# A decoder layer in fp32: buffers of the MLP taken strictly in turn, a longer tail by token blocks, and a shorter inverse root

## The chip, the cores and the metric

The kernel runs on one core of a Trainium2 chip. The core has five engines that work side by side: TensorE (PE in the profile, with the weight load PEld beside it), VectorE (DVE), ScalarE (ACT), GpSimd (POOL) and SyncE (SP), which here issues the transfers. Each engine works its own instructions off in the order in which they were written for it. The metric is the device time of one execution in microseconds, lower is better; the time before is the median of three runs.

## The reference

One decoder layer on 2048 tokens of width 1024, in fp32:

```python
# token mixing: projection, differential attention + mLSTM heads, output projection
x1 = x + rmsnorm(mix(rmsnorm(x, g_mix_pre)), g_mix_post)
# channel mixing: hidden width 4096, squared ReLU
h  = rmsnorm(x1, g_mlp_pre)
u  = square(relu(h @ w_up))
y  = x1 + rmsnorm(u @ w_down, g_mlp_post)

def rmsnorm(x, g):
    return x * lax.rsqrt(mean(x * x, axis=-1) + 1e-6) * g
```

The change touches the end of the token mixing (the inverse root in the output projection) and the whole of the channel mixing.

## The kernel before, in words

**Products.** An fp32 operand is split into two fp32r parts, high and low: ScalarE makes the high part by a cast, VectorE the low part by a subtraction, and a product is three matmuls (high·high, high·low, low·high) of 128x128 by 128x512, all issued by `product` at line 962. The two matrix products of the MLP are done in Strassen's manner with seven smaller products each, numbered 1 to 7.

**Output projection** (`out_proj`). Per block of 128 tokens `project` multiplies, `residual` normalises twice with `rsqrt_act` and writes x1 to DRAM, and `spread` transposes the result and forms the seven right operands `B` of the up projection; those that don't stay in SBUF go through two buffers `hl` to DRAM (`Bd`).

**Up projection** (`MlpUp`). For two halves of the tokens (g) and eight pairs of row blocks each, the products go in the order 1, 2, 6, 7, 5, 3, 4, always for two row blocks together. Weights are loaded into `wr`, split into `w`, multiplied into the PSUM tiles `A` and `B`, squared into `u` (with `s` as a helper) and stored to DRAM as `ud`. The pools hold 5 `s`, 15 `u`, 14 `wr`, 6 `w`, 4 `A` and 4 `B`. `Rotation` (line 820) hands out tiles from up to two pools in turn; within one pool the scheduler may give a new tile any buffer that is free.

**Down projection** (`mlp_down`). The products go in the order 1, 6, 5, 3, 2, 7, 4, each over 16 blocks j. For each block `operands(i, j)` loads `ar` (line 1169) from `ud`, casts it to `ao` (ScalarE, line 1171), subtracts for the low part of `ao` (VectorE, line 1146, the helper `tt`); `right(i, j)` loads one to four pieces `br` of the weights (line 1152), combined by `tt` where there is more than one (none, 2, 1, none, none, 1, 3 subtractions or additions for products 1, 6, 5, 3, 2, 7, 4); the result is cast to `bo` (line 1175) and its low part subtracted. Then eight token blocks b get three matmuls each, into the eight PSUM tiles `pd`: 24 matmuls a block. With a product's last block, `take` empties each `pd`: a copy on ScalarE (line 1186) for products 1, 6, 5, 3, an addition to `y` on VectorE for 2, 7, 4. Buffers: 4 `ar`, 5 `ao`, 5 `bo`, 14 `br`, 6 `x1`. All loads of the stage are issued by SP in one queue, in the order of the program as the scheduler wrote it.

**The end.** The last four blocks of the last product (`TAIL`) are done the other way round: all four operand pairs are made first, then each token block gets its 12 matmuls at once, followed by its own `take`, `sumsq` (line 1199: square on ScalarE with its sum; line 1200: times the gain on GpSimd) and `finish`: sum of the two halves `ss`, `rsqrt_act` (lines 180 to 186), scaling (line 1223 on ScalarE with the addition of x1 on GpSimd, line 1224; line 1226 on VectorE for the other half) and the stores of the output (line 1227).

## Time and profile before

| | us |
|---|---|
| median of three runs (2589.5, 2590.0, 2593.72) | 2590.0 |
| the profiled execution | 2593.08 |
| its span | 2591.3 |
| mean granted clock of TensorE | 0.97 of full speed |
| TensorE busy | 2433.5 (94%) |
| VectorE busy | 1456.9 (56%) |
| ScalarE busy | 1057.5 (41%) |
| GpSimd busy | 436.1 (17%) |

The span is the stretch between the first and the last event of the profiled execution, and its own time lies 1.8 us above it. The up projection fills about 1344 to 1937 us, the down projection the rest.

### The profile page before, as it was taken

How to read it: one execution, taken by the hardware profiler on the slowest of the kernel's cores; microseconds unless marked ns; L12 is line 12 of the kernel's file. 1: busy time of each engine (PE TensorE's matmuls, PEld its weight loads, DVE VectorE, ACT ScalarE, POOL GpSimd, SP SyncE). 2: the span in 40 equal slices, each digit the busy share in tenths (PEclk: the TensorE clock that was granted, in tenths of full speed). 3: DMA queues.
4: the chain of work that ended last, by engine and by line, in shares of the span. 5: the costliest groups of instructions: out<-in, count | busy, mean ns of one | idle time of the engine just before them, and what ended most of it. 6: DMA issues, size and time to landing. Idle time of an engine off the chain costs nothing.

```text
span 2591.3 us, 34685 instructions
## 1 busy us (share of the span) xinstructions
PE 2433.5 (94%) x12030; PEld 2042.8 (79%) x12030; DVE 1456.9 (56%) x3180; ACT 1057.5 (41%) x2103; POOL 436.1 (17%) x723
## 2 busy tenths in 40 slices
PE   8999999988888899999859999999999989999997
PEld 6888889986667778888648888888878878887876
DVE  4483441026657688566656666666665433333886
ACT  7210112326656677544424434444442332332433
POOL 0002222105635354423200000000000000000323
PEclk9999999989889899999979999999999999999999
DMA  9323442267543543255864436834468545444773
GB/s 318 126 80 94 117 126 68 58 141 171 146 97 93 128 116 95 90 171 183 270 217 162 158 136 234 316 139 149 156 211 313 195 150 187 146 164 154 295 273 106
DMA packets 296752, 424.35 MB, mean 164 GB/s; under 512 B 23585, under 2 KB 170417, under 8 KB 295041
## 3 DMA queue, kind: packets, MB, share of 16 engines
q1 hardware_dynamic: 296224, 421.94, 50.5%
q8 instruction: 95, 1.56, 0.3%
q14 instruction: 81, 0.66, 0.1%
q0 software_dynamic: 352, 0.20, 0.1%
HBM read 283.56 MB, written 138.49 MB: 163 GB/s over the span
## 4 chain that ended last, share of the span: by engine, by line
PE 71%; DMA 14%; DVE 8%; POOL 2%; ACT 2%; issue 2%; SPq 1%; POOLq 0%; DVEq 0%; ACTq 0%
PE A L962 13%; PE pd L962 13%; PE B L962 10%; PE pp L93 7%; PE pp L95 6%; PE pp L94 6%; DMA br<-in_w_down_dram 6%; PE pv L656 2%; PE s L573 2%; DMA E<-Md 2%; PE po L95 2%; PE po L93 2%; PE po L94 2%; DMA Bd<-hl 2%; DVE ao L1146 1%
## 5 line engine op out<-in xcount | busy, mean ns | idle before, releaser
L962 PE MATMUL pd<-bo,ao 128*128 128x512 f32 x2688 | 620.2, 393 | 19.5 <-DVE y L1146 8.1
L962 PEld LDWEIGHTS pd<-bo,ao 128*128 128x128 f32 x2688 | 509.6, 190 | 129.9 <-DVE bo L1146 7.2
L962 PE MATMUL A<-B,w 128*128 128x512 f32 x1536 | 359.3, 389 | 0.0
L962 PEld LDWEIGHTS A<-B,w 128*128 128x128 f32 x1536 | 288.3, 188 | 59.7
L962 PE MATMUL B<-B,w 128*128 128x512 f32 x1152 | 274.9, 392 | 18.6 <-ACT w L1052 18.6
L93 PE MATMUL pp<-w,xT 128*128 128x512 f32 (+1 forms) x768 | 271.6, 359 | 9.2 <-ACT w L230 8.5
L94 PE MATMUL pp<-w,xT 128*128 128x512 f32 (+1 forms) x768 | 273.1, 356 | 0.0
L95 PE MATMUL pp<-w,xT 128*128 128x512 f32 (+1 forms) x768 | 271.3, 355 | 0.0
L962 PEld LDWEIGHTS B<-B,w 128*128 128x128 f32 x1152 | 218.0, 189 | 64.9 <-ACT w L1052 19.6
L1171 ACT CAST ao<-ar 128x1024 fp32r<-128x1024 f32 x112 | 117.9, 1053 | 367.2 <-PE pd L962 324.3
L1200 POOL TENSOR_TENSOR y<-y,g 128x512 f32<-128x512 f32 x32 | 47.1, 1497 | 1210.0 <-ACT jk L1199 1141.5
L1019 DVE TENSOR_TENSOR w<-wr,w 128x512 fp32r<-128x512 f32 x224 | 153.7, 687 | 148.6 <-ACT w L1052 148.1
L1146 DVE TENSOR_TENSOR ao<-ar,ao 128x1024 fp32r<-128x1024 f32 x112 | 138.9, 1240 | 140.2 <-ACT ao L1171 140.2
L573 PE MATMUL s<-K,Q 128*128 128x512 f32 (+3 forms) x640 | 191.8, 413 | 13.1 <-DVE p L577 6.3
L1052 ACT CAST w<-wr 128x512 fp32r<-128x512 f32 x224 | 138.8, 621 | 131.6 <-PE B L962 113.7
L656 PE MATMUL pv<-V,pT 128*128 128x128 f32 x1088 | 158.6, 290 | 31.4 <-ACT pT L653 22.3
L656 PEld LDWEIGHTS pv<-V,pT 128*128 128x128 f32 x1088 | 147.4, 203 | 43.9 <-ACT pT L653 25.7
L1146 DVE TENSOR_TENSOR br<-br 128x512 f32<-128x512 f32 x112 | 80.1, 722 | 160.2 <-DMA br<-in_w_down_dram 154.8
L586 ACT ACTIVATE p<-p,nm 128x128 f32<-128x128 f32 (+15 forms) x128 | 153.5, 1200 | 33.2 <-DVE nm L585 20.9
L93 PEld LDWEIGHTS pp<-w,xT 128*128 128x128 f32 x768 | 144.3, 188 | 26.0 <-ACT w L230 9.9
L577 DVE TENSOR_SCALAR_CACHE_REDUCE p<-s 128x512 f32<-128x512 f32 x192 | 128.7, 683 | 50.9 <-PE s L573 23.6
L94 PEld LDWEIGHTS pp<-w,xT 128*128 128x128 f32 x768 | 144.7, 188 | 15.2 <-DVE w L231 0.3
(248 smaller groups left out, 3636.0 us busy)
## 6 DMA issues: line engine op xcount, KB each, us to landing
ud<-u SPq DMA_DIRECT2D x224, 256.0 KB, 2.4
ar<-ud SPq DMA_DIRECT2D x112, 512.0 KB, 4.2
br<-in_w_down_dram SPq DMA_DIRECT2D x224, 256.0 KB, 4.3
wr<-in_w_up_dram SPq DMA_DIRECT2D x128, 256.0 KB, 3.1
Bd<-hl SPq DMA_DIRECT2D x40, 512.0 KB, 4.2
B<-Bd SPq DMA_DIRECT2D x10, 2048.0 KB, 13.7
Q<-Qd SPq DMA_DIRECT2D x128, 128.0 KB, 4.9
raw<-in_xT_dram SPq DMA_DIRECT2D x32, 256.0 KB, 5.0
```

What stands on the lines that cost most here:

```text
L93: nc.tensor.matmul(ps, lhs[0], rhs[0], start=first, stop=False)
L94: nc.tensor.matmul(ps, lhs[0], rhs[1], start=False, stop=False)
L95: nc.tensor.matmul(ps, lhs[1], rhs[0], start=False, stop=last)
L573: nc.tensor.matmul(ps[:, :w], Q[:, var, c, qo:qo + 128], Ks[h, j][:, c, 0:w], start=(var == 0), stop=(var == 1))
L577: nc.vector.tensor_scalar(dst, ps[:, :w], 0.0, None, op0=ALU.add, op1=ALU.max, accum_out=mx[:, c, j:j + 1])
L586: nc.scalar.activation(pc[:, :W], pc[:, :W], AF.Exp, bias=nm[:, c:c + 1], accum_out=Z[:, c:c + 1])
L656: nc.tensor.matmul(pv, pT[:, i * 128:(i + 1) * 128], Vs[h, j][:, i, :], start=(b == 0), stop=(b == nb - 1))
L962: nc.tensor.matmul(ps, l[i], r[j], start=(first and k == 0 and m == 0), stop=(last and k == n - 1 and m == 2), skip_group_check=True)
L1019: self.nc.vector.tensor_tensor(out, x, y, op=op)
L1052: self.nc.scalar.copy(w[:, 0], src)
L1146: nc.vector.tensor_tensor(out, x, y, op=op)
L1171: nc.scalar.copy(l[:, 0], u)
```

## The change

- `Rotation` no longer asks a pool for any free buffer: every place has a name of its own and one buffer, and tiles take the places strictly in turn. The new `extend` adds places of a further pool behind those there are; in the up projection the early pools' places now come first.
- The same class is now used for `s`, `u`, `B` and `ar` too.
- In the down projection the sizes become: `ao` 6 (from 5), `bo` 7 (from 5), `br` 10 (from 14), `x1` 5 (from 6), `ar` 4 as before.
- `TAIL` becomes 6.
- `rsqrt_act`: ScalarE takes the root straight from the sum of squares, with the factor and an added term (the other half's sum, or epsilon from the tile `eps`) as scale and bias; VectorE makes `v` beside it; two-input operations on 128x1 are replaced by scalar operations, which take their second and third operand as per-partition scalars. In `sumsq` the first half's sum is scaled as soon as it is there.

```diff
@@ -151,10 +151,10 @@
         hp = ctx.enter_context(ExitStack())
         hpool = hp.enter_context(tc.tile_pool(name="hp", bufs=1, side="right", reuse_waits="tile"))
         ops = {i: hpool.tile([128, 2, 4, 512], F32R, name=f"B{i}") for i in NEAR[::-1]}
-        early = [hp.enter_context(tc.tile_pool(name=n, bufs=2, side="right", reuse_waits="tile"))
+        early = [hp.enter_context(tc.tile_pool(name=n, bufs=1, side="right", reuse_waits="tile"))
                  for n in ("wre", "wqe")]
         early.append(hp.enter_context(
-            tc.tile_pool(name="psE", bufs=2, side="right", reuse_waits="tile", space=PSUM)))
+            tc.tile_pool(name="psE", bufs=1, side="right", reuse_waits="tile", space=PSUM)))
         up = out_proj(tc, a, sc, ident, ops, w_out, dn, raw, shp, late["oT"],
                       lambda: MlpUp(tc, a, sc, ops, hpool, *early))
     up.run()
@@ -173,17 +173,17 @@
     return t
 
 
-def rsqrt_act(nc, pool, y, x, n, mul, add=EPS):
-
-    v = pool.tile([128, n], F32, name=f"ra_v{n}")
-    t = pool.tile([128, n], F32, name=f"ra_t{n}")
+def rsqrt_act(nc, pool, y, x, mul, add):
+
+
+    v = pool.tile([128, 1], F32, name="ra_v")
+    t = pool.tile([128, 1], F32, name="ra_t")
+    nc.scalar.activation(t, x, AF.Sqrt, scale=mul, bias=add)
     nc.vector.tensor_scalar(v, x, mul, add, op0=ALU.mult, op1=ALU.add)
-    nc.scalar.activation(t, v, AF.Sqrt)
     nc.vector.reciprocal(y, t)
-    nc.vector.tensor_tensor(t, y, y, op=ALU.mult)
-    nc.vector.tensor_tensor(t, t, v, op=ALU.mult)
+    nc.vector.tensor_scalar(t, y, y, v, op0=ALU.mult, op1=ALU.mult)
     nc.vector.tensor_scalar(t, t, -0.5, 1.5, op0=ALU.mult, op1=ALU.add)
-    nc.vector.tensor_tensor(y, y, t, op=ALU.mult)
+    nc.vector.tensor_scalar(y, t, y, None, op0=ALU.mult)
 
 
 def phase_in(tc, a, sc, ident, cst, shared):
@@ -821,13 +821,18 @@
 
 
     def __init__(self, shape, dt, name, *pools):
-        self.new = lambda p: p.tile(shape, dt, name=name)
-        self.turn = [p for p, n in pools for _ in range(n)]
-        self.n = 0
+        self.shape, self.dt, self.name, self.places, self.n = shape, dt, name, [], 0
+        for p, n in pools:
+            self.extend(p, n)
+
+    def extend(self, pool, n):
+
+        self.places += [(pool, f"{self.name}{len(self.places) + i}") for i in range(n)]
 
     def __call__(self):
+        pool, name = self.places[self.n % len(self.places)]
         self.n += 1
-        return self.new(self.turn[(self.n - 1) % len(self.turn)])
+        return pool.tile(self.shape, self.dt, name=name, bufs=1)
 
 
 def out_proj(tc, a, sc, ident, ops, w, dn, raw, shp, oT, start_up):
@@ -871,9 +876,9 @@
                 sl = slice(hf * 512, hf * 512 + 512)
                 nc.scalar.activation(t[:, sl], po[hf], AF.Square, accum_out=s2[:, hf:hf + 1])
             s1 = so.tile([128, 1], F32, name="s1")
-            nc.vector.tensor_tensor(s1, s2[:, 0:1], s2[:, 1:2], op=ALU.add)
+            nc.vector.tensor_scalar(s1, s2[:, 0:1], 1.0 / D, EPS, op0=ALU.mult, op1=ALU.add)
             rr = so.tile([128, 1], F32, name="rr")
-            rsqrt_act(nc, so, rr, s1, 1, mul=1.0 / D)
+            rsqrt_act(nc, so, rr, s2[:, 1:2], 1.0 / D, s1)
             x1 = x1p.tile([128, D], F32, name="x1")
             for hf in range(2):
                 sl = slice(hf * 512, hf * 512 + 512)
@@ -883,7 +888,7 @@
             s3 = so.tile([128, 1], F32, name="s3")
             nc.scalar.activation(t, x1, AF.Square, accum_out=s3)
             r2 = so.tile([128, 1], F32, name="r2")
-            rsqrt_act(nc, so, r2, s3, 1, mul=1.0 / D)
+            rsqrt_act(nc, so, r2, s3, 1.0 / D, eps)
             nc.vector.scalar_tensor_tensor(t, x1, r2, g2, op0=ALU.mult, op1=ALU.mult)
             return t
 
@@ -928,6 +933,8 @@
                     parts(held[1], 4, g, c)
             return half
 
+        eps = cc.tile([128, 1], F32, name="eps")
+        nc.gpsimd.memset(eps, EPS)
         g1 = cc.tile([128, D], F32, name="g1")
         nc.sync.dma_start(g1, a["g_mix_post"].partition_broadcast(128))
         g2 = cc.tile([128, D], F32, name="g2")
@@ -991,12 +998,12 @@
                 return ctx.enter_context(self.tc.tile_pool(name=name, bufs=bufs, reuse_waits="tile", **kw))
 
             self.far = pool("far", 1)
-            self.sp = pool("sp", 5)
-            self.up = pool("up", 15)
-            self.wr = Rotation([128, 512], F32, "wr", (pool("wr", 12), 12), (wre, 2))
-            self.wq = Rotation([128, 2, 512], F32R, "w", (pool("wq", 4), 4), (wqe, 2))
-            self.psA = Rotation([128, 512], F32, "A", (pool("psA", 2, space=PSUM), 2), (psE, 2))
-            self.psB = pool("psB", 4, space=PSUM)
+            self.sp = Rotation([128, 512], F32, "s", (pool("sp", 1), 5))
+            self.up = Rotation([128, 512], F32, "u", (pool("up", 1), 15))
+            self.wr.extend(pool("wr", 1), 12)
+            self.wq.extend(pool("wq", 1), 4)
+            self.psA.extend(pool("psA", 1, space=PSUM), 2)
+            self.psB = Rotation([128, 512], F32, "B", (pool("psB", 1, space=PSUM), 4))
             for i in (5, 3, 4):
                 self.ops[i] = self.load_op(0, i)
             for g in range(2):
@@ -1054,7 +1061,7 @@
         if i == 1:
             self.A = self.up.psA()
         elif i in (2, 7):
-            self.B = self.up.psB.tile([128, 512], F32, name="B")
+            self.B = self.up.psB()
         ps = self.A if i in (1, 6, 5, 3) else self.B
         op = self.up.ops[i]
         product(self.nc, ps, lambda k: [w[:, v, k * 128:(k + 1) * 128] for v in range(2)],
@@ -1065,12 +1072,12 @@
         getattr(self, f"after{i}", lambda: None)()
 
     def snap(self):
-        s = self.up.sp.tile([128, 512], F32, name="s")
+        s = self.up.sp()
         self.nc.scalar.copy(s, self.A)
         return s
 
     def square(self, src, vec):
-        u = self.up.up.tile([128, 512], F32, name="u")
+        u = self.up.up()
         if isinstance(src, tuple):
             self.tt(u, src[0], src[1], ALU.add)
             src = u
@@ -1100,7 +1107,7 @@
 
     def after3(self):
         u21 = self.square(self.A, False)
-        s1, self.s2 = (self.up.up.tile([128, 512], F32, name="u") for _ in range(2))
+        s1, self.s2 = (self.up.up() for _ in range(2))
         self.tt(s1, u21, self.u22, ALU.add)
         self.store(5, s1)
         self.tt(u21, self.u11, u21, ALU.subtract)
@@ -1111,7 +1118,7 @@
     def after4(self):
         u12 = self.square((self.B, self.x2), False)
         self.store(2, u12)
-        s4 = self.up.up.tile([128, 512], F32, name="u")
+        s4 = self.up.up()
         self.tt(s4, u12, self.s2, ALU.subtract)
         self.store(3, s4)
 
@@ -1124,16 +1131,16 @@
         def pool(name, bufs, **kw):
             return ctx.enter_context(tc.tile_pool(name=name, bufs=bufs, reuse_waits="tile", **kw))
 
-        ar = pool("ar", 4, side="right")
-        brr = pool("brr", 8, side="right")
-        bor = pool("bor", 2, side="right")
-        aor = pool("aor", 3, side="right")
-        ao = Rotation([128, 2, 1024], F32R, "ao", (aor, 3), (pool("aol", 2), 2))
-        bo = Rotation([128, 2, 512], F32R, "bo", (bor, 2), (pool("bol", 3), 3))
-        br = Rotation([128, 512], F32, "br", (brr, 8), (pool("brl", 6), 6))
+        ar = Rotation([128, 1024], F32, "ar", (pool("ar", 1, side="right"), 4))
+        brr = pool("brr", 1, side="right")
+        bor = pool("bor", 1, side="right")
+        aor = pool("aor", 1, side="right")
+        ao = Rotation([128, 2, 1024], F32R, "ao", (aor, 3), (pool("aol", 1), 3))
+        bo = Rotation([128, 2, 512], F32R, "bo", (bor, 2), (pool("bol", 1), 5))
+        br = Rotation([128, 512], F32, "br", (brr, 8), (pool("brl", 1), 2))
         yp = pool("yp", 1)
         xo = pool("xo", 2)
-        xp = pool("xp", 6)
+        xp = pool("xp", 5)
         so = pool("so", 3)
         psD = pool("psD", 1, space=PSUM)
 
@@ -1165,7 +1172,7 @@
             return x
 
         def operands(i, j):
-            u = ar.tile([128, 1024], F32, name="ar")
+            u = ar()
             nc.sync.dma_start(u, sc["ud"][i][j].rearrange("p g t -> p (g t)"))
             l = ao()
             nc.scalar.copy(l[:, 0], u)
@@ -1193,10 +1200,14 @@
         def sumsq(b, h, c):
 
             t = y[f"{h}{c}"][:, b]
+            s = so.tile([128, 1], F32, name=f"s{h}{c}", bufs=8)
+            jk = xo.tile([128, 512], F32, name="jk")
+            nc.scalar.activation(jk, t, AF.Square, accum_out=s)
             if (b, h) not in ss:
-                ss[b, h] = so.tile([128, 2], F32, name=f"s{h}", bufs=8)
-            jk = xo.tile([128, 512], F32, name="jk")
-            nc.scalar.activation(jk, t, AF.Square, accum_out=ss[b, h][:, c - 1:c])
+                nc.vector.tensor_scalar(s, s, 1.0 / D, EPS, op0=ALU.mult, op1=ALU.add)
+                ss[b, h] = [s]
+            else:
+                ss[b, h].append(s)
             nc.gpsimd.tensor_tensor(t, t, g3[:, (c - 1) * 512:c * 512], op=ALU.mult)
 
         x1s = {}
@@ -1212,10 +1223,9 @@
         def finish(b, h):
             rows = rows_of(b, h)
             x1 = x1s.pop((b, h))
-            s = so.tile([128, 1], F32, name="ss")
-            tt(s, ss[b, h][:, 0:1], ss[b, h][:, 1:2], ALU.add)
+            add, s = ss.pop((b, h))
             rr = so.tile([128, 1], F32, name="rr")
-            rsqrt_act(nc, so, rr, s, 1, mul=1.0 / D)
+            rsqrt_act(nc, so, rr, s, 1.0 / D, add)
             for c in (1, 2):
                 sl = slice((c - 1) * 512, c * 512)
                 t = y[f"{h}{c}"][:, b]
@@ -1226,7 +1236,7 @@
                     nc.vector.scalar_tensor_tensor(t, t, rr, x1[:, sl], op0=ALU.mult, op1=ALU.add)
                 nc.sync.dma_start(out[rows, sl], t)
 
-        TAIL = 4
+        TAIL = 6
         for i in DOWN_ORDER:
             first, last = i in (1, 2, 7), i in (3, 2, 4)
             n = 16 - (TAIL if i == DOWN_ORDER[-1] else 0)
@@ -1243,7 +1253,7 @@
                     finish(j // 2, 1)
                 if i == 4 and j < 8:
                     sumsq(j, 2, 2)
-                if i == 4 and j < 6:
+                if i == 4 and j < 5:
                     load_x1(j, 2)
             if n < 16:
                 lr = [operands(i, j) for j in range(n, 16)]
@@ -1253,8 +1263,8 @@
                     take(i, b)
                     sumsq(b, 2, 1)
                     finish(b, 2)
-                    if b < 2:
-                        load_x1(b + 6, 2)
+                    if b < 3:
+                        load_x1(b + 5, 2)
 
 
 def _constants():
```

## Rows read from the trace of the kernel before

**Rows 1.** The page: busy us of each engine, share of the span, instructions.

```profile
PE 2433.5 (94%) x12030; PEld 2042.8 (79%) x12030; DVE 1456.9 (56%) x3180; ACT 1057.5 (41%) x2103; POOL 436.1 (17%) x723
```

**Rows 2.** Windows: length, busy us of PE, PEld, DVE, ACT, POOL; clock, DMA, GB/s.

```profile
1600.00:1700.00 100.00, 100.00 (x443) 82.84 (x442) 64.42 (x103) 40.22 (x72) 0.00 (x0) 1.00 0.77 294
1900.00:2000.00 100.00, 95.48 (x414) 78.63 (x414) 55.73 (x75) 37.63 (x56) 0.00 (x0) 0.98 0.83 297
2100.00:2200.00 100.00, 93.22 (x398) 76.15 (x397) 40.38 (x47) 30.41 (x42) 0.00 (x0) 0.95 0.49 169
2300.00:2400.00 100.00, 93.96 (x402) 76.77 (x401) 42.73 (x55) 30.42 (x47) 5.24 (x5) 0.96 0.49 166
2400.00:2500.00 100.00, 97.86 (x423) 79.71 (x422) 87.98 (x149) 39.57 (x79) 29.31 (x19) 0.99 0.81 300
```

**Rows 3.** Chain that ended last, a piece: start, us, work (the up stage).

```profile
1369.36 5.44 PE B L962 x24
```

**Rows 4.** Waits of PE, 1930 to 2592 us: total us, times, longest.

```profile
PE pd L962 <- DVE y L1146: 8.1, 5, 4.0
PE pd L962 <- DVE bo L1146: 6.5, 2, 5.9
```

**Rows 5.** Timeline, 2095 to 2135: start, us, engine, line, work, [idle before, releaser].

```profile
2102.19 0.68 DVE L1146 TENSOR_TENSOR bo<-br,bo 128x512 fp32r<-128x512 f32 x1
...
2102.90 5.52 SPq L1152 DMA_DIRECT2D br<-in_w_down_dram  x2
...
2107.37 0.69 DVE L1146 TENSOR_TENSOR br<-br 128x512 f32<-128x512 f32 x1 [4.50 <-DMA br<-in_w_down_dram]
...
2107.98 1.22 DVE L1146 TENSOR_TENSOR ao<-ar,ao 128x1024 fp32r<-128x1024 f32 x1
2109.12 0.69 DVE L1146 TENSOR_TENSOR bo<-br,bo 128x512 fp32r<-128x512 f32 x1
...
2123.83 11.49 PE L962 MATMUL pd<-bo,ao 128*128 128x512 f32 x38 [5.94 <-DVE bo L1146]
```

**Rows 6.** Waits of DVE, 2029 to 2117 us.

```profile
DVE br L1146 <- DMA br<-in_w_down_dram: 52.9, 14, 4.7
```

**Rows 7.** Timeline, 2376 to 2425.

```profile
2387.70 0.69 DVE L1146 TENSOR_TENSOR br<-br 128x512 f32<-128x512 f32 x1 [4.09 <-DMA br<-in_w_down_dram]
```

**Rows 8.** Timeline of the end, 2535 to 2592; TensorE's last matmuls first.

```profile
2534.77 39.83 PE L962 MATMUL pd<-bo,ao 128*128 128x512 f32 x175
...
2576.38 0.68 DVE L1146 TENSOR_TENSOR y<-y,pd 128x512 f32<-128x512 f32 x1
...
2580.07 0.68 DVE L1146 TENSOR_TENSOR y<-y,pd 128x512 f32<-128x512 f32 x1
...
2586.63 1.26 POOL L1224 TENSOR_TENSOR y<-y,x 128x512 f32<-128x512 f32 x1 [1.48 <-ACT y L1223]
```

**Rows 9.** Groups by line, 2550 to 2592: busy us, mean ns, idle before.

```profile
L1223 ACT ACTIVATE y<-y,rr 128x512 f32<-128x512 f32 x8 | 5.8, 722 | 11.1 <-DVE rr L186 9.6 <-DVE ra_v L180 1.5
...
L183 DVE TENSOR_TENSOR ra_t<-rr 128x1 f32<-128x1 f32 x8 | 5.1, 640 | 0.3
L1199 ACT ACTIVATE jk<-y 128x512 f32<-128x512 f32 x8 | 5.1, 632 | 12.3 <-DVE y L1146 8.7 <-DVE rr L182 3.6
...
L181 ACT ACTIVATE ra_t<-ra_v 128x1 f32<-128x1 f32 x8 | 1.5, 191 | 1.7 <-DVE ra_v L180 1.7
L1199 ACT ACTIVATION_READ_ACCUMULATOR jk<-y 128x1 f32 x8 | 1.5, 187 | 0.0
```

**Rows 10.** Timeline of the end, GpSimd beside VectorE.

```profile
2581.65 1.26 POOL L1200 TENSOR_TENSOR y<-y,g 128x512 f32<-128x512 f32 x1 [0.19 <-ACT jk L1199]
2581.70 0.15 DVE L185 TENSOR_SCALAR ra_t<-ra_t 128x1 f32<-128x1 f32 x1
2581.77 1.15 DVE L1146 TENSOR_TENSOR ss<-s 128x1 f32<-128x1 f32 x1
```

**Rows 11.** Waits of PE, 1180 to 1345 us.

```profile
PE tp L910 <- DVE hl L897: 21.1, 2, 20.7
```

## The prediction

> **What bounds the kernel now.** I read the engine totals first: TensorE is busy for 94% of the span, every other engine for 56% or less [rows 1]. So time can only come from places where TensorE stands, and from the end. The windows by stage say where these are: no idle time inside the up projection, one dent where the down projection takes over (1900 to 2000: 4.5 us idle, clock 0.98) and three inside it, each with TensorE's granted clock lowered beside it [rows 2]. In 2100 to 2200 us TensorE lacks 6.8 us and the clock is 0.95; in 2300 to 2400 it lacks 6.0 at 0.96; in 2400 to 2500, 2.1 at 0.99. After a stall the clock goes to the lower of its two levels (1.2 instead of 2.4 GHz) for a while, which these means contain. I price it as the window's length times the missing share: 5 us for the first dent, 4 + 1 for the second.
>
> One block of the down projection is 24 matmuls; the chain has 24 such matmuls of the up stage at 5.44 us [rows 3], so a block needs 5.44 us and one product (16 blocks) 87 us.
>
> The waits name the releasers: in the down stage TensorE waited 6.5 us for VectorE's `bo` and 8.1 for its `y` [rows 4]. The timeline shows why `bo` was late [rows 5]. VectorE works in order. Its subtraction `br<-br` belongs to a block far ahead; it waits 4.50 us for its load; that load was issued only when `bo` of the block before (2102.19 to 2102.87) had given back a `br` buffer, at 2102.90. Queued behind the waiting subtraction are `ao` (1.22) and `bo` (0.69) of the block that TensorE wants next. So `bo` frees a buffer, a load fills it, the subtraction takes it, then come `ao` and `bo`: from `bo` at 2102.19 to `bo` at 2109.12 it is 6.93, call it 7.0 us, 1.55 over TensorE's 5.44. Fourteen such waits stand in the stretch of the second product [rows 6]. Sixteen blocks times 1.55 make 25 us, against a lead of four blocks (five pairs, one in use) or 21.8 us. The 3 us missing, and something lost at the start of the stretch, appear as the 5.94 us stall at 2123.83. At 2387.70 the same subtraction, 4.09 us late, holds up `ao`, `bo` and the addition that empties `pd` [rows 7].
>
> The end is another matter: TensorE finishes at 2574.60 and the span ends at 2591.3 [rows 8], 16.7 us later.
>
> **The change part by part.** Durations are of the profiled execution, 2593.1 us; the median of the runs is 2590.0, so I sum against the first and take 3.1 off at the end.
>
> *Tail of six.* Before, TensorE gives 12 matmuls (5.44 / 24 = 0.227 us each) to a token block, 2.72 us, but the chain behind it repeats every 3.70 (`y<-y,pd` at 2576.38 and 2580.07) [rows 8]; the chain falls behind and sets the end. With 18 matmuls TensorE needs 4.08, more than 3.70: it becomes the bound, and only the last token block's chain hangs out behind 2574.60.
>
> *Inverse root.* That last chain is: addition 0.68, square 0.63 and its accumulator 0.19, root 0.19, four short operations of VectorE at 0.15, scaling on ScalarE 0.72, addition on GpSimd 1.26 [rows 8 to 10], together 4.27, with 0.3 between them 4.6, then the store's 3.4 (2587.89 to 2591.3). It ends at 2582.6: **8.7 us gained**. Were the old root kept, the chain would take at most what the last token block's took, from 2580.07 to 2587.89, 7.8 us [rows 8], and the gain would be 5.5. So the bounds are 5.5 and, with the 0.3 between the steps gone, 9. GpSimd's two instructions a block, 1.26 each [rows 8, 10], stay under 4.08, so nothing is late next there.
>
> Why the root is shorter: L183, a two-input operation on 128x1, takes 640 ns on average [rows 9]. The timeline shows what it and `ss` wait for: while GpSimd runs from 2581.65 to 2582.91, the scalar operation L185 takes 0.15, and `ss` right behind it 1.15, ending with GpSimd [rows 10]. The change turns the two-input ones into scalar ones. The Trainium skill ("SBUF — State Buffer", section "Who interferes with whom") says the same of a VectorE instruction with two SBUF inputs beside a GpSimd one that reads SBUF; but it also says that tensor_scalar can enter two-port modes and then be blocked itself, and by that the gain would lie near 5.5. L185 at 0.15 under a running GpSimd instruction speaks for the first.
>
> In the output projection the same shorter root stands in a stretch where TensorE waited 21.1 us for `hl`, whose two buffers wait for stores [rows 11]. That wait hides it: 0, at most 1 us if it is the root that ends last.
>
> *Strict turn in the up stage* (wr, w, A, B, s, u). TensorE is at 100% at 1600 to 1700 [rows 2]. A place in turn comes round after about a batch of 14 products of 12 matmuls, 38 us, so its last reader has long been done. I take 0; without that cover, a waiting `wr` load would stop SP's queue, with every `ud` store behind it, and a stall would cost what the dents show, 6 to 12 us.
>
> *Strict turn and sizes in the down stage.* `ao` goes from 5 to 6, `bo` from 5 to 7: the lead grows from four blocks to five, 27.2 us. `br` goes from 14 to 10 in strict turn: load n waits for the last reader of load n-10. Where a block has two loads, the one that stays until `bo` returns five blocks later, so the loop bo, load, subtraction, bo can go on at 7.0 us; it is bounded by 5.44 below (TensorE's pace) and 7.0 above, and I take 7.0. Sixteen blocks then cost 25 us against 27.2: the first stall goes, 6.8 + 5 = **11.8 us**. For the second and third (6.0 + 5 + 2.1 = 13.1) the lead is also longer, but what stood there was `y` queued behind a subtraction that waits for its load, and a longer lead doesn't reorder VectorE. Between 0 and 13.1 I take half, **6.5**, since both parts are of one size. `x1` at 5 instead of 6 buffers: loads issued token blocks ahead, 0.
>
> Sum: 2593.1 - 8.7 - 11.8 - 6.5 = 2566.1; less 3.1, **2563 us**, its own range 2555 to 2574.
>
> **Rivals.**
>
> *All dents go* (also the one at the change of stages, 4.5 us and 2 of clock [rows 2]): 2593.1 - 8.7 - 11.8 - 13.1 - 6.5 - 3.1 = 2550. For it: every dent is VectorE's order, and the shorter run-ahead of loads may clear it. Against: a longer lead lets VectorE make more operands at the change of stages, ahead of the up stage's last work.
>
> *The strict turn changes nothing in the loop*, and its fewer buffers eat what the sixth pair gives; only the tail counts: 2593.1 - 8.7 - 3.1 = 2581. For it: the load is issued 0.03 us after `bo` ends, so the buffer's return sets the pace, and there are fewer buffers now.
>
> *Slower: ten `br` buffers instead of fourteen spread the 7.0 us loop over more blocks.* The products with three and four loads a block get three or two blocks of run-ahead, so a load waits for a `bo` only three or two blocks back. With n looped blocks in a row the stall is 1.55 n - 27.2. It eats the tail's gain and the first stall's (8.7 + 6.8) from n = 28 on. If all 32 blocks of two products loop, it is 22.4 us and 5 more of clock: 2593.1 - 8.7 - 6.8 + 22.4 + 5 - 3.1 = 2602; with ten more of the last product, 15.5 on top, 2617, and the six pairs for the tail come late too. Against: with more loads a block VectorE's queue may have `ao` and `bo` in front of the subtraction, and then nothing is lost.
>
> *No change*: about 28 looped blocks, the point just worked out, give 2585 to 2595.
>
> **How the numbers follow.** My forecast 0.44, all dents gone 0.13, tail only 0.15, no change 0.08, slower 0.20. A measurement of this kernel can tell about 0.2%, 5 us, from no change. Faster: 0.44 + 0.13 + 0.15 = 0.72; same 0.08; slower 0.20. The range 2548 to 2604 takes in every case but the far part of the slower one and the edge of the second.
>
> **What the profile after would show.** The tail: `y<-y,pd` 4.1 us apart, the last one starting right after TensorE's end, and the span ending some 8 us behind it; no 128x1 operation of VectorE over 0.2 us. The first stall: no wait of TensorE for `bo` and a clock of 1.00 in that hundred microseconds. The loop: if VectorE's waits for `br` loads in the second product go well above 53 us [rows 6], or appear in products that had none, the slower case is there. The prediction fails if the six-block tail finds its pairs missing (TensorE idle in the last 60 us), or if the strict turn stops TensorE in the up stage.

## The result and the profile after

The changed kernel takes 2563.3 us in the median of four runs (2556.62 to 2563.49) against 2590.0: a ratio of 0.9888, 95% interval 0.9869 to 0.9906. Its profiled execution took 2563.28 us with a span of 2561.4, 29.9 less than before. The forecast was 2563; several of its terms were not what they seemed, and they happened to balance.

The engine totals of the page after, to set beside [rows 1]:

```profile
PE 2425.0 (95%) x12030; PEld 2040.0 (80%) x12030; DVE 1456.0 (57%) x3132; ACT 1065.2 (42%) x2103; POOL 440.1 (17%) x724
```

The windows of the changed kernel by the same hundred microseconds as [rows 2] (columns as there):

```profile
1900.00:2000.00 100.00, 100.00 (x443) 82.84 (x442) 53.65 (x69) 38.98 (x55) 0.00 (x0) 1.00 0.77 275
...
2100.00:2200.00 100.00, 100.00 (x443) 82.84 (x442) 37.67 (x44) 37.70 (x54) 0.00 (x0) 1.00 0.47 165
...
2300.00:2400.00 100.00, 95.22 (x414) 78.36 (x413) 55.17 (x84) 36.22 (x70) 25.73 (x16) 0.98 0.49 169
2400.00:2500.00 100.00, 99.38 (x438) 81.68 (x437) 79.28 (x124) 35.46 (x55) 13.22 (x8) 1.00 0.89 315
...
2520.00:2530.00 10.00, 9.05 (x32) 6.88 (x33) 5.97 (x11) 2.64 (x7) 0.94 (x1) 0.83 0.00 1
```

Two dents are gone, with their clock: the one at the change of stages (1900 to 2000) and the first one inside the down projection (2100 to 2200). The one at 2300 has shrunk from 6.0 to 4.8 us idle and from 4 to 2 us of clock, the one at 2400 from 2.1 to 0.6. The last line is a new one: a short stall and 0.83 of the clock, 1.7 us, where the six-block tail begins. TensorE's waits in the down stage are to be set beside [rows 4]. One more row of before belongs there, the dent at the change of stages:

```profile
PE pd L962 <- DVE u L1019: 4.5, 1, 4.5
```

After:

```profile
PE pd L969 <- DVE y L1153: 4.8, 1, 4.8
PE pd L969 <- DVE ao L1153: 2.9, 2, 2.6
PE pd L969 <- DVE s L1207: 0.6, 1, 0.6
```

`bo` and `u` no longer appear; `y` stays; `ao` is new. VectorE's waits in the second product (16 blocks, 2024 to 2111 us), beside [rows 6]:

```profile
DVE br L1153 <- DMA br<-in_w_down_dram: 24.2, 14, 3.2
```

The waits for `br` loads have more than halved, from 52.9 us in 14. The timeline of this stretch shows another order of the work (same columns as [rows 5]):

```profile
2087.24 0.69 DVE L1153 TENSOR_TENSOR br<-br,br 128x512 f32<-128x512 f32 x1 [1.32 <-DMA br<-in_w_down_dram]
2087.85 0.68 DVE L1153 TENSOR_TENSOR bo<-br,bo 128x512 fp32r<-128x512 f32 x1
2087.96 0.93 SPq L1159 DMA_DIRECT2D br<-in_w_down_dram  x2
...
2090.13 1.23 DVE L1153 TENSOR_TENSOR ao<-ar,ao 128x1024 fp32r<-128x1024 f32 x1 [1.60 <-ACT ao L1178]
...
2092.16 0.69 DVE L1153 TENSOR_TENSOR br<-br,br 128x512 f32<-128x512 f32 x1 [0.80 <-DMA br<-in_w_down_dram]
2092.77 0.68 DVE L1153 TENSOR_TENSOR bo<-br,bo 128x512 fp32r<-128x512 f32 x1
```

What matters is the order. Before, VectorE's queue held subtraction, `ao`, `bo`, and the two loads went out 5 us apart. Now `bo` stands directly behind the subtraction, the two loads go out within 1 us, beginning as the subtraction ends, and `ao` is done while they are under way. From `bo` to `bo` it is 4.92 us here, under TensorE's 5.44; before it was 6.93.

These are single steps, and of different blocks: VectorE works ahead, so at that time before it made the `bo` of product 6, and now it makes those of product 5. Counted over the traces, the mean step from `bo` to `bo` in the 16 blocks of product 6 was 6.65 us before and is 5.61 now. Before, 20 to 11 subtractions for blocks further on were already done when a `bo` of product 6 was made; now it is 4 or fewer.

The end (timeline; TensorE's last matmuls first), beside [rows 8]:

```profile
2520.61 1.40 PE L969 MATMUL pd<-bo,ao 128*128 128x512 f32 x3 [2.58 <-DVE ao L1153]
...
2522.35 30.77 PE L969 MATMUL pd<-bo,ao 128*128 128x512 f32 x130 [0.34 <-DVE ao L1153]
...
2549.08 0.69 DVE L1153 TENSOR_TENSOR y<-y,pd 128x512 f32<-128x512 f32 x1 [0.48 <-PE pd L969]
...
2553.16 0.69 DVE L1153 TENSOR_TENSOR y<-y,pd 128x512 f32<-128x512 f32 x1 [0.48 <-PE pd L969]
```

TensorE ends at 2553.12, the last addition starts at 2553.16, token blocks are 4.08 us apart, and the span ends 8.3 us after TensorE instead of 16.7. But the tail begins with TensorE waiting 2.9 us for `ao`: the pairs were not there. The prediction had named this as a sign that it fails.

### The profile page after: what moved, and what is told of

Same layout as the page of the kernel before. It is cut to its first block, busy times and chain, and to the rows that moved or that the text cites. A ratio compares the mean times of both kernels' runs of the same rounds, so it can differ in the third digit from the quotient of the medians.

```text
span 2561.4 us, 34625 instructions
## 1 busy us (share of the span) xinstructions
PE 2425.0 (95%) x12030; PEld 2040.0 (80%) x12030; DVE 1456.0 (57%) x3132; ACT 1065.2 (42%) x2103; POOL 440.1 (17%) x724
## 4 chain that ended last, share of the span: by engine, by line
PE 76%; DMA 11%; DVE 6%; POOL 2%; ACT 2%; issue 2%; SPq 0%; POOLq 0%; DVEq 0%; ACTq 0%
PE pd L969 16%; PE A L969 14%; PE B L969 10%; PE pp L93 7%; PE pp L94 7%; PE pp L95 7%; DMA br<-in_w_down_dram 3%; PE pv L656 3%; PE s L573 3%; PE po L93 2%; DMA E<-Md 2%; PE po L94 2%; PE po L95 2%; PE tp L651 2%; DMA wb<-Wd 1%
## 5 line engine op out<-in xcount | busy, mean ns | idle before, releaser
L969 PE MATMUL pd<-bo,ao 128*128 128x512 f32 x2688 | 613.8, 390 | 8.3 <-DVE y L1153 4.8
L93 PEld LDWEIGHTS pp<-w,xT 128*128 128x128 f32 x768 | 144.4, 188 | 25.9 <-ACT w L230 8.7
L94 PEld LDWEIGHTS pp<-w,xT 128*128 128x128 f32 x768 | 144.5, 188 | 15.2 <-DVE w L231 0.3
L95 PEld LDWEIGHTS pp<-w,xT 128*128 128x128 f32 x768 | 144.3, 188 | 15.1
```

The source lines that it names most:

```text
L93: nc.tensor.matmul(ps, lhs[0], rhs[0], start=first, stop=False)
L94: nc.tensor.matmul(ps, lhs[0], rhs[1], start=False, stop=False)
L95: nc.tensor.matmul(ps, lhs[1], rhs[0], start=False, stop=last)
L969: nc.tensor.matmul(ps, l[i], r[j], start=(first and k == 0 and m == 0), stop=(last and k == n - 1 and m == 2), skip_group_check=True)
```

## The experiments

All runs were timed beside the kernel before. The table gives each ratio with its 95% interval, and three stretches of each profiled execution, read from its timeline: the output projection (from the first to the last matmul into `po`), the down stage (from the first to the last matmul into `pd`; 112 blocks at 5.44 us would be 609.3) and the end (from there to the end of the span). The stages are compared and not the spans: the part ahead of the output projection, which no experiment changes, took between 1068.4 and 1079.8 us in these profiled executions (e7 and e12 have the two longest).

| kernel | ratio | output projection | down stage | end |
|---|---|---|---|---|
| before | 1 | 210.7 | 639.6 | 16.7 |
| changed | 0.9888 [0.9869, 0.9906] | 207.0 | 622.1 | 8.3 |
| e2: new root alone | 0.9945 [0.9932, 0.9957] | 207.1 | 635.8 | 10.9 |
| e3: strict turn alone | 0.9906 [0.9891, 0.9921] | 210.7 | 618.7 | 16.7 |
| e8: as e3, `ar` free | 0.9909 [0.9896, 0.9922] | 210.8 | 622.3 | 16.6 |
| e9: strict turn, down stage alone | 0.9946 [0.9933, 0.9959] | 210.7 | 627.5 | 17.0 |
| e14: strict turn, up stage alone | 0.9960 [0.9949, 0.9972] | 210.8 | 629.8 | 16.7 |
| e5: changed, buffers free | 0.9934 [0.9920, 0.9947] | 207.0 | 637.5 | 8.3 |
| e4: changed, tail of four | 0.9868 [0.9852, 0.9883] | 207.1 | 616.6 | 10.9 |
| e7: changed, old root | 0.9925 [0.9912, 0.9938] | 210.8 | 625.3 | 12.4 |
| e10: turn and root, old sizes, tail of four | 0.9875 [0.9863, 0.9888] | 207.1 | 616.3 | 10.9 |
| e15: changed, 14 `br` | 0.9871 [0.9857, 0.9886] | 207.1 | 619.5 | 8.2 |
| e1: before, `br` work on GpSimd | 0.9932 [0.9919, 0.9945] | 210.8 | 622.9 | 16.9 |
| e12: e10, `br` work on GpSimd | 0.9879 [0.9861, 0.9896] | 207.0 | 618.0 | 10.9 |

The theory to be tested is the prediction's own: the first dent goes because the sixth `ao` lengthens the lead, while VectorE's loop goes on at 7.0 us; the tail of six and the root together set the end. The main rival: the turn itself does it.

**e3, the strict turn alone** (the changed class, used everywhere as in the change; all sizes, root and tail as before):

```diff
-        ao = Rotation([128, 2, 1024], F32R, "ao", (aor, 3), (pool("aol", 2), 2))
+        ao = Rotation([128, 2, 1024], F32R, "ao", (aor, 3), (pool("aol", 1), 2))
...
-        self.up = pool("up", 15)
+        self.up = Rotation([128, 512], F32, "u", (pool("up", 1), 15))
```

> The kernel before with nothing changed but the strict turn, all numbers of buffers as before (ao 5, bo 5, br 14, x1 6), tail of four and old root. Theory A (sizes: the dents go because the lead grows from four blocks to five): both the dent at the change of stages and the first one inside the down projection stay, 2585 to 2592 us (ratio 0.998 to 1.001). Rival B (turn: the order in which buffers come back sets where VectorE waits): the 1937 dent (4.5 + 2 us) and the first (6.8 + 5 us) go, 2570 to 2578 (ratio 0.993 to 0.995).

0.9906, the rival's side, and more than it expected. The waits of TensorE in its down stage:

```profile
PE pd L967 <- DVE y L1151: 4.9, 3, 2.0
PE pd L967 <- DVE bo L1151: 0.6, 1, 0.6
```

No wait for `u`, nearly none for `bo`: with five `ao` and five `bo`, as before, both dents are gone. The down stage is 20.9 us shorter. VectorE's waits for `br` loads have fallen much less than in the changed kernel: in 2024 to 2111 us they still sum to 41.9 us, in 17. What has changed is the order behind them and the pace: product 6 takes 6.08 us a block, for 6.65, and the lead lasts.

The order goes with the turn in all the traces. While VectorE makes the `bo` of products 6 and 5, the kernels with free buffers in the down stage (before, e2, e14) have subtraction, `ao`, `bo` in a row 17 or 18 times and subtraction, `bo`, `ao` never (e5: 16 and 3 times). The kernels with the strict turn there (changed, e3, e4, e7, e8, e9, e10, e15) have the second order 12 or 13 times and the first 4 to 10 times.

**e5, the new sizes, root and tail with free buffers** (the class and the pools as before, in both stages):

```diff
-        ao = Rotation([128, 2, 1024], F32R, "ao", (aor, 3), (pool("aol", 1), 3))
+        ao = Rotation([128, 2, 1024], F32R, "ao", (aor, 3), (pool("aol", 3), 3))
```

> The changed kernel with its new numbers of buffers, tail of six and new root, but tiles taken from any free buffer as before instead of in turn (up and down stage). Theory A (sizes): 2560 to 2566, as the changed kernel, no dent at the change of stages nor in the second product. Rival B (turn): the dents of 1937 and 2117 come back, 6.5 and up to 11.8 us: 2570 to 2582.

0.9934, rival B. Its waits:

```profile
PE pd L964 <- DVE y L1148: 9.8, 3, 4.7
PE pd L964 <- DVE u L1021: 6.9, 1, 6.9
PE pd L964 <- DVE ao L1148: 1.6, 2, 1.4
PE pd L964 <- ACT y L1188: 1.3, 1, 1.3
```

The stall at the change of stages is longer than before (6.9 for 4.5 us, both in the row for `u`); in 2100 to 2200 TensorE still lacks 2.9 of its former 6.8 us (the rows for `ao` and for ACT). Product 6 takes 6.35 us a block. So the longer lead does part of what the prediction asked of it in the first dent, but the other dent is worse, and the down stage takes 637.5. Beside e2's 635.8, which has the same root and neither turn nor sizes, the sizes and the longer tail gave the down stage nothing.

**e9 and e14, the turn by stage; e8, all but `ar`.** e9 has the strict class only for `ar`, `ao`, `bo`, `br`; e14 only for `wr`, `w`, `A`, `B`, `s`, `u`. e8 was meant to be e14, but the class there served the down stage's `ao`, `bo` and `br` as well, so that only `ar` stayed free; its expectation describes a kernel that it was not, and its time says only that `ar` makes no difference.

> The kernel before with the strict turn in the up stage alone (wr, w, A, B, s, u). Theory A: the turn acts through the loads br, ar and the operands of the down stage, so this changes nothing: ratio 0.998 to 1.002, the dents of 1937 and 2117 as before. Rival B: the dent at the change of stages is one of the up stage's tiles u and B and goes with their order: 6.5 us, ratio 0.997 to 0.998.

> The kernel before with the strict turn in the down stage alone (ar, ao, bo, br), numbers of buffers as before. Theory A: all of the 0.991 that the strict turn in both stages gave: ratio 0.990 to 0.992. Rival B: all but the dent at the change of stages: 0.993 to 0.994.

> The kernel before with the strict turn for the up stage's buffers alone; ar, ao, bo and br are taken as before (in the run called e8 the class was changed for all, so there ao, bo and br went in turn too, and only ar did not). Theory A: the turn of the up stage removes the dent at the change of stages (4.5 us and 2 of clock) and nothing else, the first dent of the down stage stays: ratio 0.997 to 0.998, down stage 633 us from first to last matmul. Rival B: the up stage's turn alone makes the first dent go as well: ratio 0.991 to 0.993, down stage 620.

The turn in the down stage alone (e9) took 12.1 us off the down stage and left the wait for `u` at 4.5: 0.9946, rival B's side. The turn in the up stage alone (e14) took off 9.8, removed that wait and left 5.8 us of wait for `bo`. The two sum to 21.9, together they give 20.9 (e3); the ratios too add up, 0.54% and 0.40% to 0.94%. So each turn removes the dent that lies in its own stage's buffers. e14 went beyond its expectation (629.8 for 633): its other idle time did not fall (15.2 us, for 14.9 before), so the rest lies in the granted clock, which the windows show as 0.97 for 0.95 (2100 to 2200) and 0.98 for 0.96 (2300 to 2400).

The dent at the change of stages is an order on VectorE as well. Before:

```profile
1940.94 0.68 DVE L1019 TENSOR_TENSOR u<-B,s 128x512 f32<-128x512 f32 x1
...
1941.68 6.62 PE L962 MATMUL pd<-bo,ao 128*128 128x512 f32 x21 [4.52 <-DVE u L1019]
```

and in e14

```profile
1936.34 11.95 PE L980 MATMUL pd<-bo,ao 128*128 128x512 f32 x52
...
1937.05 0.68 DVE L1037 TENSOR_TENSOR u<-B,s 128x512 f32<-128x512 f32 x1
```

The reading of the last `B` tile, for which TensorE waits, stood behind three `bo` of the down stage before and began 6.0 us after the first matmul into `pd` (1934.95); in e14 it comes ahead of them, 0.7 us after that matmul, and TensorE goes on without a wait.

**e2, the new root alone:**

```diff
-    nc.vector.tensor_scalar(v, x, mul, add, op0=ALU.mult, op1=ALU.add)
-    nc.scalar.activation(t, v, AF.Sqrt)
+    nc.scalar.activation(t, x, AF.Sqrt, scale=mul, bias=add)
+    nc.vector.tensor_scalar(v, x, mul, add, op0=ALU.mult, op1=ALU.add)
...
-    nc.vector.tensor_tensor(y, y, t, op=ALU.mult)
+    nc.vector.tensor_scalar(y, t, y, None, op0=ALU.mult)
```

> The kernel before with nothing changed but the inverse root (four-block tail, old buffers). Theory A: the old chain's 3.70 us a token block came from two-input 128x1 operations that wait for GpSimd; with scalar operations VectorE needs 2.55, GpSimd 2.55 and ScalarE 1.83 us a token block, all under TensorE's 2.72 (12 matmuls), so the end comes some 8.3 us after TensorE's last matmul instead of 16.7: 8 us faster, ratio about 0.997, and the dents stay as they are. Rival B: the longer tail is what made TensorE the bound; with four blocks the chain still falls behind and the root gives only one chain's worth, 2 to 3 us (ratio 0.999).

0.9945, some 14 us, more than theory A's 8. By the table: 5.8 us at the end (10.9 behind TensorE, not the 8.3 of theory A), 3.8 in the down stage and 3.6 in the output projection. In that last stretch (TensorE's waits, 1070 to 1290 us) the kernel before has

```profile
PE tp L807 <- DVE ra_t L185: 1.4, 1, 1.4
PE po L93 <- ACT p L811: 1.3, 3, 0.5
PE tp L910 <- DVE t L887: 0.9, 1, 0.9
PE po L95 <- DVE p L812: 0.3, 1, 0.3
```

and e2

```profile
PE tp L910 <- DVE s L874: 0.8, 1, 0.8
```

3.9 us of waits against 0.8: TensorE did wait there, longest for VectorE at an operation of the root (`ra_t`, 1.4 us), in the steady part of the projection, which lies before the wait for `hl` that was to hide it. That wait is hardly shorter in exchange: 21.1 us before, 20.9 in the changed kernel.

**e7, the changed kernel with the old root** (the same lines the other way round):

> The changed kernel with the old inverse root, all else as changed. Theory A: the root is worth one chain at the end (3 us) as long as the tail has six blocks (18 matmuls, 4.08, over the old chain's 3.70), and 5 to 6 us in the seventh product's last-but-one stage, where eight finishes run on a VectorE that is 88% busy: 2569 to 2573, ratio 0.991 to 0.993. Rival B: only the chain at the end: 2566, ratio 0.990.

0.9925, theory A by the number; the places differ: 4.1 us more at the end, 3.2 in the down stage and 3.7 in the output projection. Without the new root the six-block tail ends 12.4 us after TensorE; with the new root and four blocks it is 10.9 (e2, e4, e10); with both, 8.3. Either alone gets 4.3 or 5.8 of the 8.4 us. The end of e7:

```profile
2564.93 0.68 DVE L1151 TENSOR_TENSOR y<-y,pd 128x512 f32<-128x512 f32 x1
...
2569.11 0.68 DVE L1151 TENSOR_TENSOR y<-y,pd 128x512 f32<-128x512 f32 x1
```

The old chain repeats every 4.18 us here, not every 3.70 as in the four-block tail: it still falls behind 18 matmuls (4.08), and TensorE has ended at 2565.6 when the last token block's addition begins.

**e4, the changed kernel with a tail of four:**

```diff
-        TAIL = 6
+        TAIL = 4
```

> The changed kernel with a tail of four blocks instead of six, all else as changed. Theory A: with the new root the chain of a token block (VectorE and GpSimd 2.55 us) keeps up with 12 matmuls (2.72), so the end stays some 8.3 us behind TensorE, while TensorE no longer finds operand pairs missing when the tail begins (2.9 us, and 1.7 of clock): 2558 to 2561 us, ratio to the changed kernel 0.998 to 0.999, to the kernel before 0.988. Rival B: the six-block tail is needed; the chain falls behind by about 1 us a token block and the time is 5 to 8 us longer, 2568 to 2571.

0.9868; the two intervals overlap, so the times don't decide between four and six. The traces do, in parts: the down stage is 5.5 us shorter, since no pair is missing (TensorE's only wait there is `y`, 4.8), and the end 2.6 longer. Theory A was wrong about the end staying at 8.3: 12 matmuls take 2.72 us and the chain does not quite keep up. In its timeline of the end,

```profile
2540.12 1.30 POOL L1234 TENSOR_TENSOR y<-y,x 128x512 f32<-128x512 f32 x1
2541.38 1.75 POOL L1211 TENSOR_TENSOR y<-y,g 128x512 f32<-128x512 f32 x1
...
2543.09 1.29 POOL L1234 TENSOR_TENSOR y<-y,x 128x512 f32<-128x512 f32 x1
2544.34 1.71 POOL L1211 TENSOR_TENSOR y<-y,g 128x512 f32<-128x512 f32 x1
```

GpSimd is at work without a gap, and its multiplication takes 1.71 to 1.75 us where [rows 10] have 1.26: 2.96 us a token block, which is now the bound.

**e10, strict turn and new root with the old sizes and a tail of four:**

> The kernel before with strict turn and new root, but the old numbers of buffers (ao 5, bo 5, br 14, x1 6) and the tail of four. Theory A: the two add (23 and 14 us of span), and the new sizes and the six-block tail gave nothing or cost: 2553 to 2559, ratio 0.985 to 0.987, below the changed kernel's 0.989. Rival B: the sixth pair and the longer tail are worth what was predicted of them; without them 2566 or more, ratio 0.990 or above.

0.9875, theory A's side: no slower than the whole change. What the change added beyond turn and root, the sixth and seventh operand buffers and the longer tail, paid for by four `br` buffers, came to nothing that can be measured; by its trace the down stage would be 5.8 us shorter without them and the end 2.6 longer.

**e15, the changed kernel with 14 `br` buffers** (and 3 `x1` for 5):

```diff
-        br = Rotation([128, 512], F32, "br", (brr, 8), (pool("brl", 1), 2))
+        br = Rotation([128, 512], F32, "br", (brr, 8), (pool("brl", 1), 6))
...
-        xp = pool("xp", 5)
+        xp = pool("xp", 3)
```

> The changed kernel with 14 br buffers as before instead of 10, in strict turn, and x1 at 3 instead of 5 to make room. Theory A (the slower rival of the prediction, in small): with four loads a block ten buffers reach only two blocks ahead, so that the last product's operands come every 6.9 us and the six-block tail finds two pairs missing; with 14 the stall before the tail (2.9 us and 1.7 of clock) goes: 2557 to 2560, ratio 0.986 to 0.987, no wait of TensorE for ao in the last 60 us. Rival B: the sixth ao buffer, which is given back only when block 9 ends, makes the last pair late, whatever br does: 2563, ratio 0.989, the wait stays.

Its waits in the down stage:

```profile
PE pd L969 <- DVE y L1153: 4.9, 2, 4.0
PE pd L969 <- DVE ao L1153: 0.6, 1, 0.6
```

The wait for `ao` falls from 2.9 to 0.6 us and the down stage from 622.1 to 619.5, with the same six `ao`. So it was mainly the ten `br` buffers that made the pairs late, not the sixth `ao`. The ratio, 0.9871, does not by itself stand clear of the changed kernel's.

**e1 and e12, the `br` work on GpSimd:**

```diff
-            tt(x, x, y, ALU.subtract)
+            op = (nc.gpsimd if i in (6, 5, 7) else nc.vector).tensor_tensor
+            op(x, x, y, op=ALU.subtract)
             if i in (6, 4):
                 z = load(1, 1)
-                tt(x, x, z, ALU.add)
+                op(x, x, z, op=ALU.add)
```

> The kernel before with the subtractions and additions of br for products 6, 5 and 7 done by GpSimd instead of VectorE, nothing else. Theory A: the stalls come from VectorE's queue, where a br operation that waits for its load stands ahead of ao and bo; on GpSimd, which is idle there, it holds up nothing: the two dents at 2117 and 2388 (6.8 + 5 and 6.0 + 5 us) go, 2567 to 2573, ratio 0.991 to 0.993. Rival B: the loop runs through the load and the buffer, whatever engine subtracts, and GpSimd's longer instruction and its sharing with VectorE lengthen it: 2590 or more, ratio 0.999 to 1.005.

0.9932. Timeline of e1 in the second product:

```profile
2086.61 0.68 DVE L1146 TENSOR_TENSOR bo<-br,bo 128x512 fp32r<-128x512 f32 x1
2086.66 1.78 POOL L1159 TENSOR_TENSOR br<-br 128x512 f32<-128x512 f32 x1 [3.67 <-DMA br<-in_w_down_dram]
2088.47 0.80 SPq L1152 DMA_DIRECT2D br<-in_w_down_dram  x2
...
2090.91 1.22 DVE L1146 TENSOR_TENSOR ao<-ar,ao 128x1024 fp32r<-128x1024 f32 x1 [3.61 <-ACT ao L1172]
2092.05 0.68 DVE L1146 TENSOR_TENSOR bo<-br,bo 128x512 fp32r<-128x512 f32 x1
```

GpSimd now waits for the load, 3.67 us, and nobody stands behind it; `bo` follows `bo` at 5.44, TensorE's pace (mean over product 6: 5.43). Buffers, loads and their number are those of before, and both dents it was aimed at are gone (TensorE 100% busy at 2100 to 2200 and at 2300 to 2400). What stalled TensorE was the work queued on VectorE behind a waiting subtraction. One thing more has changed here, as in e3: the two loads of a block go out within 1 us of each other. The runs don't take this apart from the order on VectorE. Left are the 4.5 us for `u` and 4.9 near 2400 to 2500.

> Strict turn and new root with the old numbers of buffers and the tail of four (as in the run e10), and the br operations of products 6, 5 and 7 on GpSimd. Theory A: what is left of the dents near 2350 and 2450 (4.1 us idle and 2 of clock) is y queued behind a waiting br operation and goes: 2551 to 2557, ratio 0.983 to 0.986. Rival B: GpSimd beside VectorE's two-input ao and bo costs as much as it frees: 2560 or more, ratio 0.987 to 0.990.

0.9879, rival B by the number. On top of turn and root GpSimd's help buys nothing: the dent of 2300 to 2400 goes, but near 2466 a single wait of 5.8 us appears, at the end of product 7. The timeline there:

```profile
2464.77 0.69 DVE L1166 TENSOR_TENSOR br<-br,br 128x512 f32<-128x512 f32 x1 [2.94 <-DMA br<-in_w_down_dram]
2465.38 0.68 DVE L1153 TENSOR_TENSOR y<-y,pd 128x512 f32<-128x512 f32 x1
...
2466.20 10.01 PE L969 MATMUL pd<-bo,ao 128*128 128x512 f32 x36 [5.84 <-DVE y L1153]
```

This is the same pattern: the addition to `y` stands behind a `br` operation of product 4, which was left on VectorE and waits for its load.

## Why the prediction came out as it did

- **The reading of the stalls** (a far-ahead `br` subtraction that waits for its load, with `ao`, `bo` and `y` behind it on VectorE) was right: e1 takes just that work off VectorE and the two dents go. The dent at the change of stages is an order on VectorE too (e14), as the rival "all dents go" had supposed.
- **The first stall, 11.8 us, "goes"**: it went, but the step that was to do it failed. The prediction let the loop "go on at 7.0 us" and trusted the longer lead. The strict turn alone, with the old numbers of buffers, removes the stall (e3), since product 6 takes 6.08 us a block for 6.65; the new sizes without the turn leave 2.9 of 6.8 us idle and the change of stages worse (e5). Nor was the loop bounded by 5.44 from below: single steps take 4.4 to 5 us. In the changed kernel, 5.61 a block, the lead is hardly used. The prediction's arithmetic was off for the stall itself too: 16 steps of 6.65 lose 19 us, not 25. Why the scheduler writes `bo` ahead of `ao` and both loads close together when buffers are taken in turn stays open, and so does what part the shorter run-ahead of the subtractions has; the traces show only that they come together.
- **The strict turn in the up stage, "I take 0"**: it removed the dent at the change of stages, 4.5 and 2 us (e14). That cover was sought for a loss; a gain was not allowed for, though the dent stood in [rows 2].
- **The second and third dent, half of 13.1**: 4.8 and 0.6 us idle and 2 of clock are left, so 5.7 went, for 6.5. Half was a split between two bounds, so that it came out near is luck. The reason given, `y` behind a waiting subtraction that a longer lead doesn't reorder, is what the wait of 4.8 still shows:

```profile
2369.75 0.69 DVE L1153 TENSOR_TENSOR br<-br,br 128x512 f32<-128x512 f32 x1 [4.47 <-DMA br<-in_w_down_dram]
2370.36 0.68 DVE L1153 TENSOR_TENSOR y<-y,pd 128x512 f32<-128x512 f32 x1
...
2371.18 29.20 PE L969 MATMUL pd<-bo,ao 128*128 128x512 f32 x121 [4.78 <-DVE y L1153]
```

- **The end, 8.7 us**: 8.4. But the premise that 18 matmuls, 4.08 us, are enough to make TensorE the bound was wrong: with the old root the chain takes 4.18 there (e7), so it needs the root too, and the 5.5 given as the least that the tail brings was 4.3. The new root alone brings 5.8 us (e2).
- **The scalar operations** run beside GpSimd, as [rows 10] had shown for L185; groups by line of VectorE in the end of the changed kernel:

```profile
L184 DVE TENSOR_SCALAR ra_t<-rr,ra_v 128x1 f32<-128x1 f32 x8 | 2.2, 272 | 0.3
L182 DVE TENSOR_SCALAR ra_v<-s,s 128x1 f32<-128x1 f32 x8 | 1.7, 213 | 4.8 <-ACT jk L1205 4.7
L186 DVE TENSOR_SCALAR rr<-ra_t,rr 128x1 f32<-128x1 f32 x8 | 1.7, 213 | 0.2
...
L185 DVE TENSOR_SCALAR ra_t<-ra_t 128x1 f32<-128x1 f32 x8 | 1.2, 154 | 0.3
```

  154 to 272 ns, for 640 on average and up to 1150 before. Those with one scalar read from SBUF (L182, L186) take some 60 ns more than L185, the one with two (L184) some 120, so the sign "no 128x1 operation of VectorE over 0.2 us" was missed by a little. In the last token block L183 to L186 run from 2554.95 on, while GpSimd's multiplication runs from 2554.67 to 2555.93, and none waits for its end. The Trainium skill's warning ("SBUF — State Buffer", section "Who interferes with whom") that a tensor_scalar can enter a two-port mode and then be blocked by GpSimd did not come true for these 128x1 tiles. Its rule for two SBUF inputs did, by the `ss` of 1.15 us in [rows 10].
- **The root in the output projection, "0, at most 1 us"**: 3.6. The cover named, the wait for `hl`, lies behind the steady part in which TensorE waited for it.
- **The slower rival**, ten `br` buffers, was real in small: the last product's pairs came late to the tail, 2.9 us and 1.7 of clock, and with 14 buffers most of it goes (e15). It was given as a rival and as a sign of failing, not as a term. The sign named for it in the second product, waits for `br` well above 53 us, did not come: they are 24.2.

Put together from the trace: end 8.4, first dent 11.8, second and third 5.7, change of stages 6.5, output projection 3.6, less 4.6 for the tail's beginning: 31.4 us, against 29.9 of span; the difference lies in the rough pricing of the clock. The forecast of the profiled execution was 2566.1 and it took 2563.3: some 10 us of gains left out stand against 4.6 of loss left out and a first pricing that was 1.1 too high. In the median the two agree more closely only because the 3.1 us that lay between profile and median before are not there after. So the direction and the two main places, first dent and end, were forecast for reasons that hold in part; that the time was met to within 1 us is luck.

## What to carry to other kernels

When an engine that works in order waits for a transfer, look at what stands behind the waiting instruction, and change its place before adding buffers: the same load, waited for by an idle engine or with the urgent work ahead of it, cost next to nothing here (e1, e3), while the added `ao` and `bo` buffers bought nothing that could be measured (e10). How buffers are handed out can change the order in which the scheduler writes the instructions; a change that looks like mere bookkeeping deserves a term of either sign. Before pricing a short chain at nothing, check where it recurs and that the wait meant to hide it covers that place.

## What the runs showed of the hardware

GpSimd's 128x512 multiplication takes 1.26 us in [rows 10] and 1.71 to 1.75 us in e4 where it overlaps VectorE's scaling of 128x512, an instruction with two SBUF inputs. That scaling takes 0.75 us in the changed kernel's last token block (at 2555.97, as GpSimd's multiplication ends) and up to 1.74 in e4:

```profile
2548.98 1.74 DVE L1236 SCALAR_TENSOR_TENSOR y<-y,rr,x 128x512 f32<-128x512 f32 x1 [0.34 <-POOL y L1211]
```

So in these rows each engine is slowed by the other, and with it GpSimd's 2.96 us a token block set the end of the four-block tail.
